# Two layers of short convolution and mLSTM: another hand-written order around the third weight unit

## Chip, cores, metric

One core of one Trainium2 chip. The metric is the device time of one execution in microseconds (us). Engines are named as in the profile: PE (TensorE), PEld (its weight loads), DVE (VectorE), ACT (ScalarE), POOL (GpSimd), SP (the queue that issues the loads).

## What is computed

The reference is a small decoder trunk in float32: 1024 tokens and 16 meta tokens, width 1024, two layers. The change lies in the first layer, a gated short convolution; the second is a matrix-memory (mLSTM) layer that the diff does not touch.

```
u = rmsnorm(h, norm_w[0])
b_gate, c_gate, xin, z = split(u @ w_in, 4)          # w_in: 1024 x 8192
y = causal depthwise conv, width 3, of (c_gate * xin)
h = h + (silu(z) * b_gate * y) @ w_out               # w_out: 2048 x 1024
```

## The kernel before

Every large product is made of *units*. A unit holds two 128-column tiles of a weight matrix over all 1024 rows of it. For each of 16 column tiles j there are two units: `xc{j}` (the columns of xin and of the C gate) and `zb{j}` (those of z and of the B gate). So xc0, zb0, xc1, zb1 are the first four.

A unit is cut into four blocks (upper and lower half of the rows, first and second tile), and so are the activations u (halves of the rows, halves of the 1040 tokens). From xc1 on, the 2x2 block product is done with seven products (`P1` to `P7`, Winograd's scheme) instead of eight, on sums and differences of the blocks. Every float32 operand is scaled by a power of two and split in two float16 parts, hi and lo; a product takes three passes (hi·hi, hi·lo, lo·hi), which makes 24 matmuls of 128x128 with 260 columns for each of P1 to P7. The hi part is made on ACT, the lo part on DVE. xc0 and zb0 use eight plain products instead (`product`: P1, P2, A21, P4 against P1, P2, B12, P3 of u), since the sums of u are being made meanwhile: `u.t1` to `u.t4` are its four block differences (T1 to T4), `u.hi("P7", 1)` and `u.lo("P7", 1)` split one of them.

A unit's preparation runs in stages, one for each call of `step()`: stage 0 loads the two halves of the unit, takes the largest magnitude of each half on DVE (L130), broadcasts the larger over the partitions with a PE matmul against the identity (L94, tile `all_...`), makes the scale with five small DVE instructions (L105 to L126), and makes the sums on POOL (L211, four instructions). Stages a, b, c, d split the operands (hi at L139 on ACT, lo at L144 on DVE: `whia`/`wloa` to `whid`/`wlod`): a serves P1 and P2, b serves P6 and P5, c serves P7 and P3, d serves P4. `take(name)` runs the stages of a unit that are still missing.

`project` does one unit's seven products, with two PSUM tiles x and w: P1 in x, P2 in w, P6 on top of x, P5 afresh in w, P7 on x, P3 on w, P4 on x. Between them results leave PSUM by ACT copies (`copy_out`, L619) or DVE instructions (`axpy`, L834). w can be opened for P5 only when the L834 instruction after P2 has read it.

The order of instructions comes from two sources. Up to the end of zb0 it is written out by hand for all engines (`by_hand`, L660 to L793): there each engine runs its instructions in the order of the text. Behind that, a planner orders each engine's queue with its own cost estimates, with the order of the text as priority; it may also slip instructions from behind the hand-written part into its gaps. On the chip each queue then runs in its fixed order: an instruction that waits holds up all behind it on its engine. PSUM tiles (`acc_tile`) come from one pool of four, and `all_...` tiles from the same pool.

The last part of the hand-written order handles zb0: d11, d12, d21, d22 are its four block results (tile `d_zb` in the trace). z is the Silu of d11 and d12 (ACT), y the convolution with three taps (ACT, then two on DVE), y times z goes to POOL, and g = d21, d22 times y (L1030, DVE) closes column tile 0, hand-ordered too. In the same stretch xc1 (`following`) is prepared.

Of the kernel before, what the change touches and what calls it, by code (L numbers as in the profile page):

```python
# [12 lines left out]
AF = mybir.ActivationFunctionType  # L13
# [46 lines left out]
def pair(t, *idx):  # L60
    return tuple(x[idx] for x in t)
# [3 lines left out]
def trunk(ctx, tc, hx, wci, wco, wqk, wv, woz, wg, wmo, cw, nw, gb, hnw, fnw, out):  # L65
    nc = tc.nc
# [223 lines left out]
    def step():  # L290
        next(prep, None)
# [7 lines left out]
    def take(key):  # L299
        ready(key)  # L300
        return units.pop(key)
# [83 lines left out]
    def feed(accs, w, u, nk, fresh):  # L385

        for kt in range(nk):
            for q, (a, b) in enumerate(PASSES):
                for acc, cols in accs:
                    mm(acc, w(kt)[a], u(kt, cols)[b], fresh and kt == 0 and q == 0, kt == nk - 1 and q == 2)  # L390
                    fill()
# [185 lines left out]
    cw_sb = const.tile([P, NJ, 3], F32, name="cw_sb")  # L577
# [6 lines left out]
    with l0:  # L584
# [6 lines left out]
        def v2(t):  # L591
            return t.rearrange("p (c n) -> p c n", c=2)

        def acc_tile(name):
            return psum.tile([P, 2, 512], F32, tag="acc", name=name)
# [4 lines left out]
        def spans(acc):  # L600
            return [(acc[:, c, :QW], slice(c * QW, (c + 1) * QW)) for c in range(2)]

        def used(acc):
            return acc[:, :, :QW]
# [5 lines left out]
        cx = row.tile([P, 2 + TOK], F32, name="cx")  # L610
# [3 lines left out]
        def row_tile(tag, name):  # L614
            return row.tile([P, 2, TH], F32, tag=tag, name=name)

        def copy_out(acc, ds, tag, name):
            t = cpp.tile([P, 528], F32, tag="cp", name=f"{tag}_{name}")[:, :TH]
            nc.scalar.activation(v2(t), used(acc), AF.Identity, scale=ds)  # L619
            return t  # L620


        with ExitStack() as n0:
# [3 lines left out]
            u = Operands(  # L627
                [
                    (q, {"B12": pair(b12, slice(None), slice(2 * r, 2 * r + 2)), **dict(zip(OPS, uo0[r]))})
                    for r, q in enumerate(u32.quarters)  # L630
                ],
                u32.spare,
            )
# [20 lines left out]
            def product(acc, a, b, fresh):  # L654
                feed(
                    spans(acc), lambda kt: pair(unit.ops[a], slice(None), slice(kt * P, (kt + 1) * P)),
                    lambda kt, c: pair(u.dst[kt // 2][b], slice(None), kt % 2, c), 4, fresh,
                )

            with by_hand(mybir.EngineType.PE):  # L660
# [27 lines left out]
                unit = units["xc0"]  # L688
# [68 lines left out]
                unit = take("zb0")  # L757
                d11, d12 = acc_tile("d11_zb0"), acc_tile("d12_zb0")
# [7 lines left out]
                y = yh.rearrange("p a n -> p (a n)")  # L766
                zt = row_tile("xz", "z_0")
                following.largest((0,))
                u.t3()
                u.hi("P7", 1)  # L770
                nc.scalar.activation(y, cx[:, 2:], AF.Identity, scale=cw_sb[:, 0, 2:3])
                nc.scalar.activation(v2(zt[:, 0]), used(d11), AF.Silu, scale=unit.ds)
                following.largest((1,))
                d21 = acc_tile("d21_zb0")
                product(d21, "A21", "P1", True)
                product(d21, "P4", "P2", False)
                spreading["psum"] = lambda name: acc_tile(name)[:, 0]
                following.spread()
                for k in (1, 2):
                    nc.vector.scalar_tensor_tensor(out=y, in0=cx[:, 2 - k : 2 - k + TOK], scalar=cw_sb[:, 0, 2 - k : 3 - k], in1=y, op0=ALU.mult, op1=ALU.add)  # L780
                nc.scalar.activation(v2(zt[:, 1]), used(d12), AF.Silu, scale=unit.ds)
                for i in range(2):
                    nc.gpsimd.tensor_tensor(out=yh[:, i], in0=yh[:, i], in1=zt[:, i], op=ALU.mult)
                u.lo("P7", 1)
                d22 = acc_tile("d22_zb0")
                product(d22, "A21", "B12", True)
                product(d22, "P4", "P3", False)
                step()
                u.t4()
                step()  # L790
                u.hi("P4", 2)
                step()
                u.lo("P4", 2)  # L793

        spreading["psum"] = lambda name: acc_tile(name)[:, 0]
# [3 lines left out]
        def project(name, on11, on12, on21, on22):  # L799

            unit = take(name)
            ops = unit.ops
            ds = unit.ds
            step()
            step()

            def run(x, acc, fresh):
                i = OPS.index(x)
                feed(spans(acc), lambda kt: pair(ops[x], slice(None), slice(kt * P, (kt + 1) * P)), lambda kt, c: pair(uo0[kt // 2][i], slice(None), kt % 2, c), 4, fresh)

            x = acc_tile(f"x_{name}")
            w = acc_tile(f"w_{name}")
            run("P1", x, True)
            p1 = copy_out(x, ds, "p1", name)
            run("P2", w, True)
            on11(w, ds, p1)
            step()
            run("P6", x, False)
            u2 = copy_out(x, ds, "u2", name)
            run("P5", w, True)  # L820
            p5 = copy_out(w, ds, "p5", name)
            step()
            run("P7", x, False)
            u3 = copy_out(x, ds, "u3", name)
            nc.gpsimd.tensor_tensor(out=u3, in0=u3, in1=p5, op=ALU.add)
            on22(u3)
            run("P3", w, False)
            on12(w, ds, u2)
            step()
            run("P4", x, False)  # L830
            on21(x, ds)
# [4 lines left out]
        def conv_tile(j, g, between):  # L836
            xt = row_tile("xz", f"x_{j}")
            c2 = []
            project(
                f"xc{j}",  # L840
                lambda acc, ds, p: axpy(xt[:, 0], acc, ds, p),
# [19 lines left out]
            def gate(i, acc, ds, p):  # L861
# [3 lines left out]
                if i == 1:  # L865
                    nc.gpsimd.tensor_tensor(out=g[:, 1], in0=b2[0], in1=yh[:, 1], op=ALU.mult)

            project(
                f"zb{j}",
                lambda acc, ds, p: gate(0, acc, ds, p),  # L870
# [143 lines left out]
        for j in range(NJ):  # L1014
# [4 lines left out]
            if j == NJ - 1:  # L1019
                early = pool(ahead, "ahead", side="right")  # L1020
                for un in range(2):
                    unit = units[f"co3_{un}"]
# [113 lines left out]
        for un in range(2):  # L1136
            unit = units[f"co3_{un}"]
# [18 lines left out]
        u = Operands(  # L1156
            [(q, {x: pair(uo, slice(None), i, slice(2 * r, 2 * r + 2)) for i, x in enumerate(OPS)}) for r, q in enumerate(u32.quarters)],
            u32.spare,
        )
# [370 lines left out]
    def q_or_k(hd, which, ip=None):  # L1530
# [20 lines left out]
        def meta_k(ops):  # L1551
            pm = s_tile(f"km{hd}")[:, :96]
            meta_products(ops, pm)
            meta_keys(pm, f"k32_{hd}")

        return project(
            f"{'qk'[which]}{hd}",
            lambda unit: qkv,
# [703 lines left out]
```

## Time and profile before

| what | value |
|---|---|
| median of 3 runs | 1943.84 us (1938.95 to 1944.48) |
| the profiled execution's own time | 1929.85 us |
| its span, first to last instruction | 1928.1 us |
| mean granted TensorE clock | 0.971 of full |
| PE busy | 1762.4 us, 91% of the span |
| DVE busy | 1491.6 us, 77% |
| POOL busy | 1040.4 us, 54% |
| ACT busy | 951.5 us, 49% |

The shares are means over the whole execution. The stretch that the diff touches lies at some 60 to 130 us of 1928, so it has to be read there. Times below are counted from the span's start.

### The profile page before, as it was taken

The numbers are of one execution on the slowest core, as the hardware profiler recorded it, in microseconds if no ns is written. First come the engines' busy times: TensorE is split into PE (matmuls) and PEld (weight loads), VectorE is DVE, ScalarE is ACT, GpSimd is POOL, SyncE is SP. The second block draws the span as 40 slices with busy tenths as digits, with TensorE's granted clock in tenths as the row PEclk, the third lists the DMA queues.
The fourth block names the chain that finished last, engine by engine and source line by source line (L and its number), as shares of the span: only waits on it lengthen the run. The fifth ranks groups of instructions, "written<-read, shape, count | busy, mean of one in ns | idle before, by whom it ended". The sixth has DMA issues, their size and how long they took to land. (4 is left out here: it accounts for less than half of the span.)

```text
span 1928.1 us, 34947 instructions
## 1 busy us (share of the span) xinstructions
PE 1762.4 (91%) x14577; PEld 1284.6 (67%) x14577; DVE 1491.6 (77%) x2114; ACT 951.5 (49%) x1300; POOL 1040.4 (54%) x766
## 2 busy tenths in 40 slices
PE   7799999998999898888899988999989999899977
PEld 6588788887888787774585444864448644396446
DVE  6966886678667876978878788688886878878786
ACT  5444543444344433555656464465544555455545
POOL 2444484546544545865565457544576444765454
PEclk8899999999999999999999999999999999999998
DMA  4211111111111111000211111101111111110102
GB/s 145 90 54 59 52 45 67 45 56 56 46 65 45 58 53 47 29 23 12 69 48 33 55 57 56 50 23 66 53 50 52 33 55 53 50 56 34 44 23 88
DMA packets 34102, 100.84 MB, mean 52 GB/s; under 512 B 5388, under 2 KB 7692, under 8 KB 33944
## 3 DMA queue, kind: packets, MB, share of 16 engines
q1 hardware_dynamic: 33944, 98.61, 15.5%
q8 instruction: 114, 1.87, 0.4%
q14 instruction: 44, 0.36, 0.1%
HBM read 94.36 MB, written 4.24 MB: 51 GB/s over the span
## 5 line engine op out<-in xcount | busy, mean ns | idle before, releaser
L376 PEld LDWEIGHTS <-u_hi 128*128 128x128 f16 (+1 forms) x2228 | 152.5, 99 | 17.0 <-issue 10.5
L864 POOL TENSOR_TENSOR y<-y,z 128x520 f32<-128x520 f32 x30 | 43.1, 1436 | 87.8 <-DVE y L857 76.0
L376 PEld LDWEIGHTS <-u_lo 128*128 128x128 f16 x1108 | 80.1, 100 | 5.5 <-issue 0.9
L211 POOL TENSOR_TENSOR s_xc<-r_xc 128x512 f32<-128x512 f32 x15 | 20.0, 1334 | 91.1 <-DVE m_xc L88 50.2
L376 PEld LDWEIGHTS <-whic_zb 128*128 128x128 f16 x480 | 48.3, 101 | 27.6 <-issue 18.7
L1849 POOL TENSOR_TENSOR n<-n,den 128x512 f32<-128x512 f32 x32 | 43.2, 1381 | 41.1 <-DVE den L1847 35.0
L376 PEld LDWEIGHTS <-whia_xc 128*128 128x128 f16 x544 | 53.8, 99 | 13.8 <-ACT whia_xc L139 3.9
L376 PEld LDWEIGHTS <-whia_zb 128*128 128x128 f16 x544 | 52.6, 97 | 7.9
L376 PEld LDWEIGHTS <-whib_xc 128*128 128x128 f16 x480 | 47.1, 98 | 15.0 <-issue 7.2
L931 POOL TENSOR_TENSOR h<-h,u_mo 128x512 f32<-128x512 f32 x30 | 45.1, 1515 | 20.2 <-ACT u_mo L1895 9.8
L130 DVE TENSOR_REDUCE mx_xc<-r_xc 128x1 f32<-128x1024 f32 x32 | 38.7, 1213 | 19.6 <-DMA r_xc<-in_wci_dram 19.6
L376 PEld LDWEIGHTS <-whib_zb 128*128 128x128 f16 x480 | 46.5, 97 | 7.2
L376 PEld LDWEIGHTS <-whic_xc 128*128 128x128 f16 x480 | 46.5, 97 | 7.1
L931 POOL TENSOR_TENSOR h<-h,u_co 128x520 f32<-128x520 f32 (+2 forms) x31 | 45.5, 1471 | 10.1 <-ACT u_co L985 7.4
L1834 POOL TENSOR_TENSOR ssv<-ssv,sqn 128x512 f32<-128x512 f32 x24 | 40.5, 1689 | 18.7 <-ACT sqn L1832 17.4
L211 POOL TENSOR_TENSOR s_zb<-r_zb 128x512 f32<-128x512 f32 x15 | 21.8, 1457 | 46.0 <-DVE wlob_xc L144 23.2
L923 DVE SCALAR_TENSOR_TENSOR h<-w_co,ds_co,h 128x520 f32<-128x520 f32 (+2 forms) x48 | 35.7, 753 | 13.3 <-POOL h L931 6.7
L144 DVE SCALAR_TENSOR_TENSOR wloc_xc<-s_xc,s_xc,whic_xc 128x1024 f16<-128x1024 f32 x15 | 31.5, 2100 | 15.1 <-ACT whic_xc L139 15.1
L130 DVE TENSOR_REDUCE mx_zb<-r_zb 128x1 f32<-128x1024 f32 x32 | 38.9, 1214 | 5.4 <-DMA r_zb<-in_wci_dram 4.7
L619 ACT ACTIVATE u_xc<-x_xc,ds_xc 128x520 f32<-128x520 f32 x30 | 20.8, 692 | 43.9 <-PE x_xc L376 43.9
L834 DVE SCALAR_TENSOR_TENSOR x<-w_xc,ds_xc,u_xc 128x520 f32<-128x520 f32 x15 | 11.4, 757 | 39.3 <-PE w_xc L376 39.3
L844 POOL TENSOR_TENSOR cx<-u_xc,x 128x520 f32<-128x520 f32 x15 | 28.3, 1890 | 23.4 <-DVE x L834 23.4
(1077 smaller groups left out, 7014.6 us busy)
## 6 DMA issues: line engine op xcount, KB each, us to landing
r_xc<-in_wci_dram SPq DMA_DIRECT2D x32, 512.0 KB, 3.5
r_zb<-in_wci_dram SPq DMA_DIRECT2D x32, 512.0 KB, 3.6
r_v<-in_wv_dram SPq DMA_DIRECT2D x16, 512.0 KB, 3.6
r_o<-in_woz_dram SPq DMA_DIRECT2D x16, 512.0 KB, 3.6
r_z<-in_woz_dram SPq DMA_DIRECT2D x16, 512.0 KB, 3.5
r_mo<-in_wmo_dram SPq DMA_DIRECT2D x16, 512.0 KB, 3.6
r_co<-in_wco_dram SPq DMA_DIRECT2D x12, 512.0 KB, 3.6
h<-in_hx_dram SPq DMA_DIRECT2D x16, 260.0 KB, 6.0
```

The costliest lines, as they stand in the source:

```text
L130: nc.vector.tensor_reduce(out=out_, in_=in_, axis=axis, op=ALU.max, apply_absolute_value=True)
L144: nc.vector.scalar_tensor_tensor(out=lo, in0=raw, scalar=s, in1=hi, op0=ALU.mult, op1=ALU.subtract)
L211: nc.gpsimd.tensor_tensor(out=o, in0=a, in1=b, op=op)
L376: nc.tensor.matmul(o, lhs, rhs, start=start, stop=stop, skip_group_check=True)
L619: nc.scalar.activation(v2(t), used(acc), AF.Identity, scale=ds)
L834: nc.vector.scalar_tensor_tensor(out=v2(dst), in0=used(acc), scalar=ds, in1=v2(addend), op0=ALU.mult, op1=ALU.add)
L844: nc.gpsimd.tensor_tensor(out=cxr[:, 1], in0=c2[0], in1=xt[:, 1], op=ALU.mult),
L864: nc.gpsimd.tensor_tensor(out=yh[:, i], in0=yh[:, i], in1=zt[:, i], op=ALU.mult)
L923: nc.vector.scalar_tensor_tensor(out=hv, in0=acc, scalar=ds, in1=hv, op0=ALU.mult, op1=ALU.add)
L931: nc.gpsimd.tensor_tensor(out=hv, in0=hv, in1=t, op=ALU.add)
L1834: nc.gpsimd.tensor_tensor(out=ssv, in0=ssv, in1=sq, op=ALU.add)
L1849: nc.gpsimd.tensor_tensor(out=n[:, vt, :], in0=n[:, vt, :], in1=den, op=ALU.mult)
```

## The change

In the hand-written order, the part that prepares xc1 while zb0's products run is rearranged. The Silu of d11 comes first on ACT, ahead of the first tap of y and of P7's hi. The two maxima of xc1 follow each other, with T3 behind them instead of between them. The Silu of d12 and xc1's stage 0 (its scale) come ahead of the two taps of y on DVE, xc1's stage a comes behind the taps, then P7's hi, T4, stage b, P4's hi. P7's lo goes from ahead of T4 to behind it, next to P4's lo. PE's own hand-written order stays d21, the broadcast, d22.

In `project`, for xc1 and zb1 alone, the two `step()` calls that prepare the next unit (stage 0 and stage a of zb1 and of xc2) move from ahead of P1 to behind P2, ahead of the step that is there already.

```
@@ -766,30 +766,30 @@
                 following.largest((0,))
-                u.t3()
-                u.hi("P7", 1)
-                nc.scalar.activation(y, cx[:, 2:], AF.Identity, scale=cw_sb[:, 0, 2:3])
                 nc.scalar.activation(v2(zt[:, 0]), used(d11), AF.Silu, scale=unit.ds)
                 following.largest((1,))
+                nc.scalar.activation(y, cx[:, 2:], AF.Identity, scale=cw_sb[:, 0, 2:3])
+                u.t3()
                 d21 = acc_tile("d21_zb0")
                 product(d21, "A21", "P1", True)
                 product(d21, "P4", "P2", False)
                 spreading["psum"] = lambda name: acc_tile(name)[:, 0]
                 following.spread()
+                nc.scalar.activation(v2(zt[:, 1]), used(d12), AF.Silu, scale=unit.ds)
+                step()
                 for k in (1, 2):
                     nc.vector.scalar_tensor_tensor(out=y, in0=cx[:, 2 - k : 2 - k + TOK], scalar=cw_sb[:, 0, 2 - k : 3 - k], in1=y, op0=ALU.mult, op1=ALU.add)
-                nc.scalar.activation(v2(zt[:, 1]), used(d12), AF.Silu, scale=unit.ds)
                 for i in range(2):
                     nc.gpsimd.tensor_tensor(out=yh[:, i], in0=yh[:, i], in1=zt[:, i], op=ALU.mult)
-                u.lo("P7", 1)
+                step()
+                u.hi("P7", 1)
+                u.t4()
+                step()
+                u.hi("P4", 2)
                 d22 = acc_tile("d22_zb0")
                 product(d22, "A21", "B12", True)
                 product(d22, "P4", "P3", False)
-                step()
-                u.t4()
-                step()
-                u.hi("P4", 2)
-                step()
+                u.lo("P7", 1)
                 u.lo("P4", 2)
@@ -801,8 +801,9 @@
             ds = unit.ds
-            step()
-            step()
+            if name not in ("xc1", "zb1"):
+                step()
+                step()
@@ -814,6 +815,9 @@
             on11(w, ds, p1)
+            if name in ("xc1", "zb1"):
+                step()
+                step()
             step()
             run("P6", x, False)
```

## Rows read from the trace of the kernel before

**Rows 1.** The page, part 1: busy us (share of the span) xinstructions.
```profile
PE 1762.4 (91%) x14577; PEld 1284.6 (67%) x14577; DVE 1491.6 (77%) x2114; ACT 951.5 (49%) x1300; POOL 1040.4 (54%) x766
```

**Rows 2.** Waits of PE, 60 to 220 us: total, times, longest.
```profile
PE all_zb L94 <- DVE m_zb L88: 10.6, 1, 10.6
```

**Rows 3.** Stretches: length, then busy time of each engine, granted clock, DMA.
```profile
core 0: us, PE busy (x) PEld busy (x) DVE busy (x) ACT busy (x) POOL busy (x), PEclk, DMA share, GB/s
72.93:77.00 4.07, 4.07 (x22) 2.96 (x22) 4.07 (x4) 0.53 (x1) 3.28 (x2) 0.58 0.00 0
80.10:90.66 10.56, 0.00 (x2) 0.03 (x1) 9.58 (x12) 3.96 (x5) 4.22 (x3) 0.67 0.72 257
91.20:94.00 2.80, 2.80 (x15) 1.95 (x13) 1.71 (x8) 1.15 (x1) 1.49 (x2) 0.51 0.22 83
100.00:220.00 120.00, 120.00 (x1076) 104.14 (x1075) 79.34 (x114) 50.07 (x60) 56.78 (x44) 1.00 0.16 54
220.00:300.00 80.00, 73.00 (x638) 62.32 (x636) 69.00 (x88) 36.59 (x43) 51.15 (x32) 0.98 0.16 51
700.00:800.00 100.00, 90.01 (x762) 75.84 (x761) 71.26 (x109) 43.74 (x57) 54.94 (x38) 0.93 0.14 42
```

**Rows 4.** Timeline of PE: start, length, instruction; in brackets idle before, releaser.
```profile
71.17 0.46 PE L94 MATMUL all_xc<-ident,m_xc 128*128 128x128 f32 x2 [2.15 <-DVE m_xc L184]
72.93 0.38 PE L376 MATMUL d_zb<-b_hi,whid_zb 128*128 128x260 f16 x2 [1.29 <-ACT z L772]
...
79.72 0.38 PE L376 MATMUL d_zb<-u_hi,wlod_zb 128*128 128x260 f16 x2
90.66 0.77 PE L94 MATMUL all_zb<-ident,m_zb 128*128 128x128 f32 x2 [10.56 <-DVE m_zb L88]
91.22 0.64 PE L376 MATMUL x_xc<-u_hi,whia_xc 128*128 128x260 f16 x2
...
95.24 0.38 PE L376 MATMUL w_xc<-u_hi,whia_xc 128*128 128x260 f16 x2
...
97.92 0.38 PE L376 MATMUL x_xc<-u_hi,whib_xc 128*128 128x260 f16 x2
...
103.51 0.27 PE L376 MATMUL x_zb<-u_hi,whia_zb 128*128 128x260 f16 x1
```

**Rows 5.** Timeline of DVE over the same stretch.
```profile
64.12 1.21 DVE L130 TENSOR_REDUCE mx_xc<-r_xc 128x1 f32<-128x1024 f32 x1
65.25 3.46 DVE L340 TENSOR_TENSOR u_a<-u_a 128x1040 f32<-128x1040 f32 x2
...
70.95 2.62 DVE L780 SCALAR_TENSOR_TENSOR y<-cx,cw_sb,y 128x1040 f32<-128x1040 f32 x2
73.49 3.47 DVE L328 TENSOR_TENSOR u_lo<-u_a,u_hi 128x1040 f16<-128x1040 f32 x2
76.89 0.28 DVE L105 TENSOR_REDUCE m_xc<-all_xc 128x1 f32<-128x128 f32 x1
...
77.96 2.40 DVE L340 TENSOR_TENSOR u_a<-u_a,spare_a 128x1040 f32<-128x1040 f32 x2
80.28 1.27 DVE L144 SCALAR_TENSOR_TENSOR wloa_xc<-r_xc,s_xc,whia_xc 128x1024 f16<-128x1024 f32 x1
...
89.03 1.42 DVE L1030 SCALAR_TENSOR_TENSOR g<-d_zb,ds_zb,y 128x520 f32<-128x520 f32 x2
...
93.75 1.28 DVE L144 SCALAR_TENSOR_TENSOR wloa_zb<-r_zb,s_zb,whia_zb 128x1024 f16<-128x1024 f32 x1 [0.95 <-ACT whia_zb L139]
...
99.75 0.75 DVE L834 SCALAR_TENSOR_TENSOR x<-w_xc,ds_xc,p_xc 128x520 f32<-128x520 f32 x1
```

**Rows 6.** Timeline of POOL.
```profile
73.72 4.39 POOL L783 TENSOR_TENSOR y<-y,z 128x520 f32<-128x520 f32 x2 [3.87 <-DVE y L780]
86.36 2.08 POOL L211 TENSOR_TENSOR s_zb<-r_zb 128x512 f32<-128x512 f32 x1 [8.25 <-DMA r_zb<-in_wci_dram]
...
90.20 1.27 POOL L211 TENSOR_TENSOR s_zb<-r_zb,r_zb 128x512 f32<-128x512 f32 x1
```

## The prediction

> **What bounds the kernel now.** I read the page first, then the waits of TensorE, then the timelines of the stretch that the diff touches, and last a table of stages. The page says that PE is the busiest engine and DVE the second [rows 1]; over the whole span DVE has room. The waits of PE between 60 and 220 us say where PE stood still: one matmul of L94, which waits 10.6 us for VectorE [rows 2]. In the table of stages the reader sees the same hole from the other side: between 80.10 and 90.66 PE does nothing while DVE is busy for 9.58 of 10.56 us; from 100 to 220 PE is busy every microsecond and DVE about two thirds [rows 3]. So this is a local knot in a kernel that PE bounds afterwards: what PE saves at 90 us is kept until 220, unless a stage hands it back.
>
> The timeline of PE shows the knot. d21 ends at 69.0. all_xc follows after 2.15 us, d22 after another 1.29 us, and d22 then runs partly at half clock (0.58 of full on the mean from 72.93 to 77.00), to about 79.9 [rows 3, 4]. Then the queue holds all_zb, the broadcast of the largest value of the *next* unit (zb1), and behind it x_xc, the first product of unit xc1 [rows 4]. On DVE, wloa_xc, the last operand of that first product, is there at about 81.5 (it is next to start at 80.28 and lasts 1.27), but the maximum of zb1 comes behind lo P4, wloc, wlod and the products g (89.03), and all_zb waits for it until 90.66 [rows 2, 3, 5]. x_xc therefore starts 9.7 us later than its data allow. A product is 2.68 us (95.24 to 97.92), and P1 took 4.02 because the clock was at half (0.51 of full, the 1.2 GHz level, from 91.2 to 94) [rows 3, 4]. From P6's start at 97.92, five products of 2.68 remain for xc1: its work would be through at **111.3**, leaving out what PE slips in for zb1. That is the mark I compare with.
>
> **The change part by part.**
>
> *Silu first, maxima ahead of T3.* No work is added or removed. DVE starts the first maximum of xc1 at 64.12; the second now follows it at once instead of after T3 (3.46) [rows 5]. So the maximum is known by 67.7 even if the maximum of zb1's first half (1.13) is slipped in as before, and PE reaches all_xc only after d21, at 69.0: the 2.15 us go. z_0's Silu, whose end d22 waited for, needs only d11, which PE multiplies before d21, so the 1.29 us go too. d22 follows at 69.4, and 48 matmuls at 2.68 us per 24 end it at 74.8 instead of 79.9. The matmuls of d21 hide the Silu on ACT; without that cover it would cost the 1.29 again.
>
> *DVE in the new order up to P1.* 64.12, plus three maxima at 1.13, the small one at 0.14, T3 at 3.46 (still beside GpSimd's sums): 71.1. The scale chain takes 1.07 (76.89 to 77.96): 72.2. The two taps of y, 2.54: 74.7. wloa, 1.25: **76.0** [rows 5]. x_xc starts there, because nothing of zb1 stands ahead of it any more. PE has been idle for 1.2 us, less than in the pauses around 70 us; I cost no half clock here. P1, P2, P6 are through at 84.0 if wlob is there.
>
> *T4, wlob, lo's.* T4 moves beside GpSimd's two products y (they start when the taps are done), so I give it the price of a pair that runs beside GpSimd, 3.46, not the 2.40 it has now. lo of P7 loses its neighbour but gets another: the load of zb1's second half waits for the buffer that wloa frees, and now lands 4.8 us after wloa's end (81.5 to 86.36), so it should land near 80.8, and GpSimd's sums of zb1 start then [rows 5, 6]. I price lo P7 at 3.4 and lo P4 at 2.3. Thus 79.5 for T4, 80.7 wlob, 84.1 lo P7, 86.4 lo P4. P6 (due 81.4) is not held.
>
> *What is late next.* P7 needs wloc, P5 needs w to be emptied by the L834 instruction after P2. Behind lo P4 on DVE come g (1.4), wloc (1.2, the same form as wloa), wlod (half as wide, 0.7), a maximum of g (1.2, the form of the other maxima) and that L834 (0.75) [rows 5]: wloc is done at 87.6 at the earliest, L834 at 91.5 if it is last, at about 82.5 if the planner slips it in as soon as P2 is done. This is the new wait, and the trace of before does not show which order it gets. Three bounds:
> - L834 last, P5 in the written order: P5 starts at 91.5, after 7.5 us of idle PE. Half clock costs what it cost in P1, 4.02 less 2.68, so 1.3. End 91.5 + 1.3 + 4 x 2.68 = 103.5: gain 7.8.
> - P7 goes ahead of P5, as the first matmuls of x_zb went ahead of P7 at 103.51 [rows 4]: 87.6 + 1.3 + 2.7 = 91.6, then three products: 99.6. Gain 11.7.
> - L834 early: P5 at 84.0, P7 at about 88.4, two more: 96.4. But zb1's first product then needs wloa_zb, which is 12 us of DVE after lo P4 (the rest above, the maximum, the scale chain, ACT's hi, its own 1.25): 98.5. Gain 12.8.
>
> I take **10 us**, between the first two, nearer the second.
>
> *Sharing with GpSimd.* A pair of DVE subtractions takes 2.40 alone and 3.47 beside GpSimd, and GpSimd's instruction 2.20 or 2.08 instead of 1.27 [rows 5, 6]; so each loses part of its speed. The Trainium skill, "SBUF — State Buffer", section "Who interferes with whom", states more: a DVE instruction with two SBUF inputs and a GpSimd instruction that reads SBUF lock each other out, and the loser stands for the whole instruction. By that rule T4 and lo P7 could each lose two GpSimd instructions of 1.27, 2.5 instead of 1.07, and the gain would be about 7 instead of 10. The trace sides with the smaller price: 3.47 is the largest of the pairs that I use.
>
> *zb1's preparations after P2, and xc2's after zb1's P2.* Two largest, four sums, one scale chain, one broadcast, operands a, and the loads (two of 512 KB each on SP) are issued later in the text. The loads wait for buffers anyway, not for their place. What they cost is cover: before, wloa of zb1 was there at 95.0, 8.5 us ahead of the first x_zb at 103.51 [rows 4, 5]; now it is about one or two ahead. From both sides: nothing if the order on DVE fits; at the far end 8.25 us, GpSimd's wait for the load of zb1 before [rows 6], which would leave a gain of 2 and is inside the range below. I take 0.5, inside the rounding to 10, since the load comes earlier here too.
>
> **The sum.** The profiled execution took 1929.85 us (span 1928.1); less 10 this is 1919.9. The median of the three runs is 1943.84, 14 us above it; the same difference taken from the median gives **1933.8**. About 0.3% (5.8 us) is what a measurement of this kernel can tell from no change.
>
> **The rivals.**
> 1. *The hole moves three products on.* all_zb is now written between P2 and P6. If the planner thinks the maximum of zb1 ready when P2 ends, all_zb stands ahead of P6. On DVE that maximum comes after lo P4, wloc, g, wlod, the maximum of g and its own 1.3: about 92.3. P6 then starts at 92.9, 1.3 lost to the clock, against 97.92: gain 3.7, time 1940. For it: exactly this happened with x_xc. Against it: DVE is full of earlier work, and the planner counts that.
> 2. *VectorE is the bound of the stage.* It is busy for 9.58 of 10.56 us [rows 3] and loses no work. If operands b and c of zb1 and a of xc2 come late too, the gain is handed back in stalls of 2 us or so each time; three of them leave 4 us: 1940. Against it: from 100 to 220 DVE is busy 79 of 120 us, so a lag of 12 us is made up in some 35. The Trainium skill, "Perfetto Trace Analysis", section "Identifying the Most-Contended Engine", says to improve the engine of highest occupancy first; taken for this stage alone, it would give no gain, 1943.8. The trace speaks against it, since PE waits here for the order of DVE's work, not for its sum.
> 3. *No effect.* The planner puts all_zb ahead of x_xc still: then x_xc starts near 91 as before, 1943.8. In the trace each broadcast comes directly ahead of the product tile written after it, so I think little of it.
> 4. *Slower.* The rest of the kernel is ordered by the planner, from times that now differ. Four stages of the first layer have an out-product of the convolution in them; the first, between 220 and 300, leaves PE idle for 7.0 us, the last, between 700 and 800, for 10.0 [rows 3], some 30 us in all if the two between are like the first (an estimate). If these idle times grew by more than half, 16 us, the change would lose; by 17 us, it ends at 1951. For it: these stages have DVE near full. Against it: all that feeds them shifts together.
>
> **How the numbers follow.** Forecast 0.68; rival 1 0.13, rival 2 0.07, rival 3 0.04, rival 4 0.08. The forecast's own range is a gain of 7 to 13, 1931 to 1937. To leave out no more than 2 in 10, the range goes up past rivals 1 and 2 and the three runs' spread (1938.95 to 1944.48) and down by as much: 1926 to 1943. Faster 0.68, same 0.24, slower 0.08.
>
> **What would show it.** Right: all_xc directly behind d21; d22 wholly at full clock; x_xc starting near 76; all_zb behind P2 or later; a PE hole of 3 to 8 us between P6 and P5 or P7 that ends with wloc_xc or the L834 x_xc; xc1's seven products through near 101. Wrong: a wait of all_zb ahead of P6, stalls of PE on wloa_zb or on operands of xc2 after 100, or more idle PE in the out-product stages of rival 4.

## The result

The changed kernel takes 1931.94 us (median of 10), the kernel before 1940.4 us (10 runs beside it): 8.5 us less, ratio 0.995 with a 95% interval of 0.993 to 0.9969. Two further comparisons gave 0.9957 (0.9939 to 0.9974; 9.2 us less) and 0.9982 (0.9963 to 1.0001; 6.0 us less); the last alone cannot be told from no change. 1933.8 was forecast, from a median that was 1943.84 then.

### The profile after

The waits of PE between 60 and 220 us (total, times, longest), against the 10.6 us of [rows 2]:

```profile
PE w_xc L376 <- DVE m_zb L88: 3.4, 1, 3.4
PE x_xc L376 <- ACT p_xc L619: 1.6, 2, 1.1
PE w_zb L376 <- DVE z L838: 1.4, 1, 1.4
PE x_xc L376 <- DVE wloc_xc L144: 0.9, 1, 0.9
PE x_xc L376 <- ACT u_xc L619: 0.8, 1, 0.8
PE w_xc L376 <- ACT p_xc L619: 0.6, 1, 0.6
PE all_xc L94 <- DVE m_xc L88: 0.4, 1, 0.4
```

The long wait is gone, and smaller ones stand in its place. (L834 of before is L838 here. The first line names m_zb, a small instruction; what P5 needs is w emptied, by the L838 instruction just ahead of it on DVE.) The timeline of PE, which answers to [rows 4]:

```profile
68.98 0.38 PE L94 MATMUL all_xc<-ident,m_xc 128*128 128x128 f32 x2
69.20 0.39 PE L376 MATMUL d_zb<-b_hi,whid_zb 128*128 128x260 f16 x2
...
74.57 0.38 PE L376 MATMUL x_xc<-u_hi,whia_xc 128*128 128x260 f16 x2
...
84.85 0.38 PE L376 MATMUL x_xc<-u_hi,whic_xc 128*128 128x260 f16 x2 [0.78 <-ACT u_xc L619]
...
86.32 0.40 PE L376 MATMUL x_xc<-u_hi,wloc_xc 128*128 128x260 f16 x2 [0.86 <-DVE wloc_xc L144]
...
92.15 0.38 PE L376 MATMUL w_xc<-u_hi,whib_xc 128*128 128x260 f16 x2 [3.42 <-DVE m_zb L88]
...
94.83 0.38 PE L94 MATMUL all_zb<-ident,m_zb 128*128 128x128 f32 x2
...
101.14 0.38 PE L376 MATMUL x_zb<-u_hi,whia_zb 128*128 128x260 f16 x2
...
111.75 0.38 PE L376 MATMUL w_zb<-u_hi,whib_zb 128*128 128x260 f16 x2 [1.44 <-DVE z L838]
...
122.48 0.38 PE L94 MATMUL all_zb<-ident,m_zb 128*128 128x128 f32 x2
```

d22 follows d21 without a pause; x_xc starts at 74.57 instead of 91.22; P7 (whic) comes ahead of P5 (whib on w); all_zb has moved behind P5; xc1's seven products are through at 101.14, where the prediction's mark for the kernel before was 111.3. zb1 then takes 21.3 us to the next broadcast, 2.6 more than seven products at 2.68. DVE, and one line of POOL, in the same stretch, for [rows 5]:

```profile
67.70 2.48 DVE L340 TENSOR_TENSOR u_a<-u_a 128x1040 f32<-128x1040 f32 x2
...
73.72 1.28 DVE L144 SCALAR_TENSOR_TENSOR wloa_xc<-r_xc,s_xc,whia_xc 128x1024 f16<-128x1024 f32 x1
74.92 4.58 DVE L340 TENSOR_TENSOR u_a<-u_a,spare_a 128x1040 f32<-128x1040 f32 x2
...
80.61 3.45 DVE L328 TENSOR_TENSOR u_lo<-u_a,u_hi 128x1040 f16<-128x1040 f32 x2
83.98 2.28 DVE L144 SCALAR_TENSOR_TENSOR wloc_xc<-s_xc,s_xc,whic_xc 128x1024 f16<-128x1024 f32 x1
...
87.98 3.45 DVE L328 TENSOR_TENSOR u_lo<-u_a,u_hi 128x1040 f16<-128x1040 f32 x2
91.35 0.75 DVE L838 SCALAR_TENSOR_TENSOR x<-w_xc,ds_xc,p_xc 128x520 f32<-128x520 f32 x1
```

```profile
73.95 4.45 POOL L783 TENSOR_TENSOR y<-y,z 128x520 f32<-128x520 f32 x2 [6.02 <-DVE y L781]
```

P2 was done at 80.1, but w is emptied only at 92.1, behind lo P7, wloc, wlod, a maximum and lo P4.

For comparing kernels I use one *stretch*: from d21's first matmul to the third all_zb, free of differences at the start of an execution. PE has the same number of matmuls in it in every kernel but the last of the table. The start of the third all_zb is called the *mark* in the expectations below. Before, then the change:

```profile
63.49 0.38 PE L376 MATMUL d_zb<-u_hi,whid_zb 128*128 128x260 f16 x2
...
162.97 0.38 PE L94 MATMUL all_zb<-ident,m_zb 128*128 128x128 f32 x2
```

```profile
63.62 0.38 PE L376 MATMUL d_zb<-u_hi,whid_zb 128*128 128x260 f16 x2
...
155.74 0.38 PE L94 MATMUL all_zb<-ident,m_zb 128*128 128x128 f32 x2
```

The stretch is 162.97 less 63.49 = 99.5 us in the profile of before, and 155.74 less 63.62 = 92.1 in that of the change: 7.4 us won. The waits of PE in it add up to 14.0 us before (2.15, 1.29 and 10.56, [rows 4]) and to 9.1 in the change. Most of the rest is clock: before, d22 took 7.0 us (72.93 to about 79.9) and P1 4.02, in part at half clock; now they take 5.4 and 2.7. Behind that, the lists of instructions of the two kernels are alike on every engine. Of the test kernels below, only "lo P7 ahead of T4" shares these lists; in all others the planner also orders some instructions of the second layer differently, from some 950 us on, so their whole times compare more than the stretch.

Ratios with the same number in the last column come from one comparison and share their runs of before; 1 is the comparison of the result.

| kernel | stretch, us | ratio of times to before (95%) | comparison |
|---|---|---|---|
| before, two profiles | 99.5, 100.7 | | |
| the change, three profiles | 92.1, 94.4, 93.0 | 0.995, 0.9957, 0.9982 | 1, 3, 4 |
| the steps alone, two profiles | 94.6, 93.0 | 0.9978 (0.996 to 0.9995), 0.9967 (0.9946 to 0.9988) | 2, 4 |
| the hand-written order alone | 101.7 | 1.001 (0.9988 to 1.0031) | 2 |
| the change without zb1's part | 97.1 | 0.9996 (0.9974 to 1.0017) | 2 |
| the change, lo P4 on GpSimd | 96.2 | 0.9974 (0.9956 to 0.9992) | 2 |
| the change, lo P7 ahead of T4 | 90.3 | 0.9965 (0.9945 to 0.9986) | 3 |
| the change, w emptied by ACT | 90.8 | 0.996 (0.9941 to 0.998) | 3 |
| both of these | 89.0 | 0.9977 (0.996 to 0.9993) | 4 |
| the steps behind P2 in all units | 93.4 for the same number of matmuls (its third all_zb stands 96 matmuls further on, at 104.2) | 1.0156 (1.0128 to 1.0184) | 3 |

### The profile page after: what moved, and what is told of

Read it like the earlier page. It is cut to its first block, busy times and chain, and to the rows that moved or that the text cites. A ratio compares the mean times of both kernels' runs of the same rounds, so it can differ in the third digit from the quotient of the medians.

```text
span 1931.2 us, 34946 instructions
## 1 busy us (share of the span) xinstructions
PE 1768.7 (92%) x14577; PEld 1285.3 (67%) x14577; DVE 1496.0 (77%) x2114; ACT 950.6 (49%) x1300; POOL 1044.0 (54%) x766
## 5 line engine op out<-in xcount | busy, mean ns | idle before, releaser
L376 PE MATMUL st<-vhi,n 128*128 128x512 f16 x96 | 32.1, 389 | 10.8 <-DVE n L1804 7.3
```

The lines of the kernel that those rows point to most:

```text
L376: nc.tensor.matmul(o, lhs, rhs, start=start, stop=stop, skip_group_check=True)
```

## The experiments

### The two parts apart

The second hunk of the diff alone (L801 to L816 of before), and the first alone.

```
-            step()
-            step()
+            if name not in ("xc1", "zb1"):
+                step()
+                step()
...
             on11(w, ds, p1)
+            if name in ("xc1", "zb1"):
+                step()
+                step()
```

> Only the second part of the change: the two preparation steps of zb1 (in xc1) and of xc2 (in zb1) come behind P2; the hand-written order is that of before. Theory A (the gain comes from taking the next unit's broadcast out of PE's way; VectorE's queue then sets P7 and P5, whatever the hand-written order): x_xc starts when wloa_xc is there, near 81.6 us instead of 91.2; the products of xc1 then run with little pause behind one another and are through near 101; time as of the whole change, 7 to 11 us faster than before, ratio 0.994 to 0.997. Rival B (the hand-written order carries the gain, since it brings d22 forward by 5 us and wloa_xc by 6): the steps alone give at most half, ratio 0.998 or above, and xc1 is through near 106.

> Only the first part: the new hand-written order; the preparation steps stay ahead of P1 in every unit. Theory A: all_zb still stands ahead of x_xc on PE and waits for the maximum of zb1, which comes behind lo P4 on VectorE, at about 91; x_xc starts near 91.5, PE's hole only begins earlier (near 75); no gain, ratio 0.999 to 1.002. Rival B: the hand-written order gives half of the gain or more, 4 us or more, ratio 0.998 or below.

The steps alone: x_xc begins at 80.47, as soon as d22 ends, and waits 0.6 us for wloa_xc. There is no long hole behind it; the planner puts some matmuls of zb1 ahead of xc1's last two products, so that the last one, P4, begins at 103.93:

```profile
82.14 0.40 PE L376 MATMUL x_xc<-u_hi,wloa_xc 128*128 128x260 f16 x2 [0.62 <-DVE wloa_xc L144]
...
90.26 0.38 PE L376 MATMUL x_xc<-u_hi,whic_xc 128*128 128x260 f16 x2 [0.78 <-ACT u_xc L619]
...
96.56 0.40 PE L376 MATMUL x_zb<-u_hi,whia_zb 128*128 128x260 f16 x2 [0.57 <-ACT whia_zb L139]
...
103.93 0.38 PE L376 MATMUL x_xc<-u_hi,whid_xc 128*128 128x260 f16 x2
```

The hand-written order alone leaves all_zb ahead of x_xc, and the hole grows, since it begins earlier and ends no sooner. Its waits of PE, 60 to 220 us:

```profile
PE all_zb L94 <- DVE m_zb L88: 16.9, 1, 16.9
```

So theory A holds for the second kernel (1.6 us slower in the medians, within the noise; stretch 1 to 2 us longer). For the first, the ratio of 0.9978 lay between the two expectations, so it was run again beside the change.

> The steps alone again, now beside the whole change on the same chip. Theory A (the hand-written order adds something: 2 to 3 us): ratio 0.997 to 0.999, above that of the change by 0.001 to 0.002. Rival B (the steps alone do all of it): ratio within 0.0008 of the change's.

> The change a third time, beside the steps alone and both edits. Ratio 0.9945 to 0.9965. The half-clock stretch behind PE's hole was there in one of two profiles and cost 2.5 us; here the stretch from d21's first matmul to the third all_zb is 92.1 us without it or 94.4 with it, within 0.5.

The steps alone came to 0.9967, the change to 0.9982, above the 0.9945 to 0.9965 expected for it, and its stretch of 93.0 lies between the two values expected. Neither theory's bound was met: the steps alone came out 0.0015 below the change. Theory A, that the hand-written order adds 2 to 3 us, is not borne out: with two and three comparisons the intervals overlap both ways, and the stretches are 94.6 and 93.0 against 92.1, 94.4 and 93.0. What the runs can tell apart is that the moved steps carry the gain and that the new order by itself carries none; whether it adds a microsecond to the steps stays open.

### zb1's part of the step move

In both conditions `("xc1", "zb1")` becomes `("xc1",)`.

> The whole change, but zb1 keeps its preparation steps (those of xc2) ahead of P1; only xc1 has them behind P2. In the changed kernel PE loses some 2.5 us inside zb1 (0.4 at all_xc, 1.4 at w_zb, 0.5 in xc2). Theory A1 (these waits come from the step move in zb1, which leaves xc2 without cover): they go, and the mark at the third all_zb comes 1 to 3 us earlier than in the changed kernel (near 153.5 instead of 155.7). Rival B1 (they come from VectorE being late, which the placing of steps does not change): all_xc stands ahead of x_zb and waits instead, the mark comes within 1 us of 155.7 or later.

Theory A1 fell; rival B1's sign came, with the mark at 160.96. With its place back ahead of x_zb, the broadcast for xc2 holds PE as the one for zb1 did before:

```profile
PE all_xc L94 <- DVE m_xc L88: 5.7, 1, 5.7
```

The stretch is 97.1, some 4 us longer than in the change, and the time cannot be told from before. The hole had only moved one unit on; of the 7 us that the change wins in the stretch, some 4 hang on zb1's condition.

### What sets the remaining hole

lo P4 to GpSimd:

```
-                u.lo("P4", 2)
+                u.lo("P4", 2, eng=nc.gpsimd)
```

> The whole change, with lo of P4 on GpSimd instead of VectorE (two subtractions; VectorE had 3.45 us for them). Theory A (the hole of PE between P7 and P5, now 3.4 us, and what follows is VectorE's queue ahead of the L838 instruction that empties w): L838 comes 3.4 us earlier, near 88, the hole shrinks to nothing, the mark at the third all_zb comes 2 to 4 us earlier than 155.7, ratio to before 0.993 to 0.995. Rival C (GpSimd is slower beside VectorE: lo of P4 and the sums of zb1 come later by 4 to 8 us, and operands b and c of zb1 with them): the hole moves into P4 or zb1, and the mark stays within 1 us of 155.7 or comes later.

Rival C by its mark, which is 159.93. DVE is not relieved: wlob, wloc and wlod last 3.17, 3.17 and 1.75 us, where they took 1.27, 2.28 and 0.74 in the change. That is 3.8 us more, for 3.45 taken off, and the L838 instruction starts at 91.92 instead of 91.35. The timelines of DVE and, below, of POOL in that kernel:

```profile
79.55 3.17 DVE L144 SCALAR_TENSOR_TENSOR wlob_xc<-s_xc,s_xc,whib_xc 128x1024 f16<-128x1024 f32 x1
...
86.03 3.17 DVE L144 SCALAR_TENSOR_TENSOR wloc_xc<-s_xc,s_xc,whic_xc 128x1024 f16<-128x1024 f32 x1
89.12 1.75 DVE L144 SCALAR_TENSOR_TENSOR wlod_xc<-r_xc,s_xc,whid_xc 128x512 f16<-128x512 f32 x1
...
91.92 0.74 DVE L838 SCALAR_TENSOR_TENSOR x<-w_xc,ds_xc,p_xc 128x520 f32<-128x520 f32 x1
```

```profile
78.55 3.09 POOL L328 TENSOR_TENSOR u_lo<-u_a,u_hi 128x1040 f16<-128x1040 f32 x1
...
84.96 3.15 POOL L328 TENSOR_TENSOR u_lo<-u_a,u_hi 128x1040 f16<-128x1040 f32 x1
```

wlob starts at 79.55, while GpSimd's instruction runs to 81.64, and ends at 82.72, about 1.1 us after it. It looks as if it stood until GpSimd had finished and then took about its usual 1.27; the profile has no line for such a stand, so this is read from the times. P7 now waits 2.7 us for wloc, and the stretch is 96.2.

Emptying w another way: in xc1 the result of P2 goes through an ACT copy, as those of the other products do, and GpSimd adds p1 to it (a second hunk, not shown, gives `on11` that sum on GpSimd).

```
             run("P2", w, True)
-            on11(w, ds, p1)
+            if name == "xc1":
+                p2 = copy_out(w, ds, "p2", name)
+                on11(p2, None, p1)
+            else:
+                on11(w, ds, p1)
```

> The whole change, and in xc1 the result of P2 leaves PSUM by an ACT copy, with the sum made on GpSimd, instead of the L838 instruction on VectorE, which came 8 us after P2's end. Theory A (PE's hole before P5 is the wait for w to be emptied): P5 follows P6 near 84, P7 follows near 87, the wait of 3.4 us is gone; what bounds next is wloa_zb, which is 0.75 us earlier (near 98), so that x_zb starts 1 to 3 us earlier than 101.1 and the mark comes 1 to 3 us earlier than 155.7. Rival B (VectorE's chain to wloa_zb and on to operands a of xc2 sets the end of the stage, whatever the order of P5 and P7): the hole only moves to x_zb, and the mark stays within 0.7 us of 155.7.

Timeline of PE:

```profile
82.94 0.39 PE L376 MATMUL x_xc<-u_hi,whib_xc 128*128 128x260 f16 x2 [1.13 <-ACT p_xc L619]
...
85.62 0.38 PE L376 MATMUL w_xc<-u_hi,whib_xc 128*128 128x260 f16 x2
...
88.31 0.38 PE L376 MATMUL x_xc<-u_hi,whic_xc 128*128 128x260 f16 x2
...
96.20 0.77 PE L94 MATMUL all_zb<-ident,m_zb 128*128 128x128 f32 x2 [3.27 <-DVE g L1038]
```

P5 follows P6 at once, so the hole ahead of P5 was the wait for w: theory A, for that step. But the planner then puts all_zb into the middle of P3, where it waits 3.3 us for g (by the profile; all_zb takes its PSUM tile from the pool of four, and g empties d21 and d22): the hole has moved on again. The mark, 156.09, is within rival B's bound; but the execution started its d21 1.7 us later than the change's, so the stretch is 90.8, 1.3 us better than the best profile of the change. The times show no difference.

### T4 and P7's lo

```
                 u.hi("P7", 1)
+                u.lo("P7", 1)
                 u.t4()
...
-                u.lo("P7", 1)
                 u.lo("P4", 2)
```

> The whole change, but P7's lo goes back ahead of T4 (behind P7's hi). Theory A (VectorE's queue, not the order of these two, sets P7 and P5; T4 first serves only P4's hi): wlob_xc comes 3.4 us later (near 84), P6 waits some 2 us, then the hole before P5 is shorter by as much; L838 is at 92 as in the change; mark within 1 us of 155.7. Rival B (the order of the two carries part of the gain): mark 2 to 4 us later, ratio 0.996 to 0.998.

Theory A by the mark (154.83), and a little better than that: P6 waits 2.5 us for wlob, the hole before P5 is gone, the stretch is 90.3. L838 did not stay at 92; it came at 88.95, ahead of the second half of lo P4. Whichever pair stands beside GpSimd's two products y is the long one (timeline of DVE; in the change it is T4, 4.58, that lasts so):

```profile
75.81 4.57 DVE L328 TENSOR_TENSOR u_lo<-u_a,u_hi 128x1040 f16<-128x1040 f32 x2
80.30 2.38 DVE L340 TENSOR_TENSOR u_a<-u_a,spare_a 128x1040 f32<-128x1040 f32 x2
```

So the new order of these two gains nothing; the order that they had before the change is at least as good.

### Both edits, and all units

> The whole change, with P7's lo back ahead of T4 and with xc1's P2 leaving PSUM by an ACT copy and a sum on GpSimd: the two edits whose stretch from d21's first matmul to the third all_zb was shorter than in the change (90.3 and 90.8 us, against 92.1 and 94.4 in two profiles of the change and 99.5 in before). Theory A (they shorten different waits, P6's and P5's): stretch 88 to 90 us, ratio to before 0.994 or below. Rival B (VectorE's sum up to operands a of zb1 is the floor, 36 us after d21's start): stretch 90 to 92 us, ratio within 0.0015 of the change's.

The stretch is the shortest of all, 89.0, as theory A said. The time is not: 0.9977, beside 0.9982 for the change in the same comparison, within rival B's bound. A stretch 3 to 5 us shorter could not be told in the whole time, which also holds a second layer in another order, so this version is not shown to beat the change.

With the condition taken out, so that every unit has its preparation steps behind P2:

> The whole change, with the preparation steps behind P2 in every unit of the convolution, not in xc1 and zb1 alone. Theory A (elsewhere nothing waits on PE's broadcasts, PE is busy throughout, so there is nothing to win; what is lost is cover): mark within 1 us of 155.7 and the lead at 780 us no larger than in the change, 3 to 7 us. Rival B (the placing is better in itself): the lead grows to 8 us or more by 780 us.

Neither theory: it is far slower, 1974.82 us against 1943.86 for the kernel before. In the stretch it does not lose (93.4 us for the same matmuls). From d21 to the first broadcast of k, in the second layer's preparation, it needs 31 us more than the change and 24 more than before (797.2 us). PE's waits between 220 and 800 us are spread over the units; short waits for w to be emptied come nine times where the change has two, though they add up to hardly more (5.9 us there):

```profile
PE w_xc L376 <- DVE x L838: 6.4, 9, 2.0
```

That PE is busy almost throughout does not make the placing of the steps free there; which of the waits costs most was not taken apart.

### The change and the kernel before once more

> The changed kernel once more, unaltered, beside the same runs of the kernel before. In its first profile it was 7.2 us ahead of before at the third all_zb, still 6.5 us ahead at 868 us, and 3.1 us behind at the end, though behind the first two units every engine has the same instructions in the same order as before. Theory A (the change acts on the first 160 us alone; what the traces differ by in the second layer is the spread between two executions): the mark comes within 0.5 us of 155.7 again, the lead at 868 us is 6 to 7 us again, and the lead at the end is another one, by 3 us or more; ratio 0.993 to 0.997. Rival D (the later start puts the second layer in a worse phase, so part of the gain is given back there each time): the end is again about 3 us behind the first profile of before, and the ratio is above 0.997.

> The kernel before once more, unaltered, for its spread. Theory A (the first profile of before ran its second layer faster than usual by chance, 1092 us from the first broadcast of k to the end, where all other runs needed 1101 to 1107 with the same order): this stretch is 1098 to 1107 us here, and the stretch from d21's first matmul to the third all_zb is 99.5 us within 1.5. Rival D (the change makes the second layer longer by 10 us): the second-layer stretch is 1092 us within 3 again.

For the change, theory A held by the ratio (0.9957), but not by the mark, which came at 158.41 and not within 0.5 us of 155.7. In the profile, its kernel ended some 3 us behind the first profile of before again, as D had it, so a profile's end and the timed runs do not say the same. This second profile has the same waits within 0.4 us, and a stretch that is 2.3 us longer. P5 takes 5.15 us there instead of 2.68, at half clock (length, then busy times, granted clock 0.50):

```profile
92.58:97.73 5.15, 5.15 (x25) 3.61 (x25) 3.70 (x5) 0.00 (x0) 0.00 (x0) 0.50 0.63 246
```

In the third profile it took 3.95 (95.16 to 99.11). So the hole's price in clock was 0, 2.5 and 1.3 us in three executions of one program.

The profiles of before needed 1092.3 and 1099.3 us from the first broadcast of k, in the second layer's preparation, to the end; those of the change 1102.1, 1102.8 and 1109.2, with the same lists of instructions there. By this the first profile of before was an unusually short one, as theory A has it, and its own span (1928.1 against 1931.2 of the change) says nothing on the change. That both values of before lie below all three of the change is not explained. The kernel with lo P7 ahead of T4, whose lists are the same there, needed 1101.2, also above both. But a lasting loss there is not in the times. From d21 to that broadcast the change is 7.6 us ahead on the mean (773.6 against 766.0), and the three timed differences, 8.5, 9.2 and 6.0, have a mean of 7.9.

## Why the prediction was right

*The knot.* Right, and as far as the runs can tell it carries the gain: PE stood behind a broadcast whose input came late. Taken away alone, it gives about the gain of the change; left in place under the new hand-written order, nothing is won.

*d22 ahead of time, wloa early.* Right in size: d22 from 69.20 to 74.57 at full clock (69.4 to 74.8 forecast), wloa at 75.0 (76.0; T3 took 2.48, not 3.46, since GpSimd's sums were nearly done), and x_xc at 74.57 without a pause, since PE began with matmuls on whia alone. But these terms were not shown to be worth anything by themselves: what the prediction took as the bounds, P7 and P5, hardly hang on them. In the steps alone wloc was done at 87.9 and w emptied at 90.3, in the change at 86.3 and 92.1. The steps alone, without the early d22 and wloa, are as fast within what the times can tell.

*The new wait.* Right in place and kind: P7 ahead of P5, held by wloc (done at 86.26, 87.6 forecast), then P5 held until the L838 instruction (done at 92.1, 91.5 forecast). The terms behind it were off against each other, and that they nearly cancelled is luck. T4 took 4.58, not 3.46; lo P4 3.45, not 2.3; wloc 2.28, not 1.2; but g fell behind L838 instead of ahead of it, and the planner put wloc, wlod and a maximum ahead of lo P4.

*Sharing with GpSimd.* Here I chose the wrong price for T4. The rule of the Trainium skill, "SBUF — State Buffer", "Who interferes with whom", by which the loser stands for the whole instruction, gave 4.9 for T4, the smaller price 3.46; measured were 4.58 in the change, and 3.17 instead of 1.27 for wlob beside a GpSimd instruction of 3.09. The traces agree with the rule where DVE came second. lo P7 took 3.45, as priced (3.4). Which of the two prices a pair paid goes with who came first: the pair of 3.47 in [rows 5] began at 73.49, ahead of GpSimd's first product at 73.72 [rows 6]; in the change that product began at 73.95, ahead of T4 at 74.92. The trace of before already held a pair above 3.47, beside GpSimd's last instruction for cx and its first sum of xc1, and I had overlooked it (timeline of DVE):

```profile
60.00 4.20 DVE L328 TENSOR_TENSOR u_lo<-u_a,u_hi 128x1040 f16<-128x1040 f32 x2 [0.28 <-ACT u_hi L320]
```

*The clock.* 1.3 us were put down for the hole before P5. That is within what three profiles showed (0, 1.3, 2.5).

*The size.* At xc1's end the gain was 10.2 us (111.3 less 101.14), as forecast. The term that was mis-sized is the cover of zb1's and xc2's preparations, put at 0.5: of the 10.3 us that the change is ahead there, counted by matmuls, zb1 gives back 2.3, at all_xc (for its maximum) and at P5 (for z on DVE), and xc2 0.6, for a copy. The first profile is left with 7.4, the three on the mean with 7.0. Rival 2 was that step, and it came true in part. That 1933.8 came so near to 1931.94 is in part luck: the gain was 1.5 us smaller than forecast, and the median of before 3.4 us lower than the one that the forecast started from. Rival 1 was avoided: all_zb came behind P5. Rivals 3 and 4 did not come.

## What to carry to other kernels

A small instruction that serves the *next* piece of work can hold a whole in-order queue: look for it where the busiest engine waits, and issue it behind the work that is ready. Do it for the units in which the lag lasts, not for all: one unit fewer moved the hole on, and with all units the kernel took 31 us more than before; numbers between were not tried. And a shift of work from VectorE to GpSimd need not free VectorE where the two then run side by side on SBUF operands: here all 3.45 us came back as longer neighbours.

## What the runs showed of the hardware

One program, after the same idle stretch of PE (a wait of 3.4 us, and one of 0.9 within the product before it), ran its next product at full clock in one execution, and partly or wholly at half clock (1.2 GHz) in two others, 2.68, 3.95 and 5.15 us for the same 24 matmuls. So a gain of a few microseconds read from one profile can be off by 2.5 from that alone.
